# Transposing B, C, x and y of the state space heads through DMA, and writing TensorE's order by hand from the third chunk on

## The chip, the cores and the metric

The kernel runs on one core of one Trainium2 chip. The metric is the device time of one launch in microseconds (us). A core has TensorE (PE in the profile; its weight loads are PEld), VectorE (DVE), ScalarE (ACT), GpSimd (POOL) and SyncE (SP), each with an instruction queue of its own that it works off in order, and 16 DMA engines. In this kernel SP issues nearly every DMA, so its queue is also the order of the transfers. Tiles in SBUF are 128 partitions wide; matmul results go to PSUM.

## The reference, cut to what matters

One layer of a hybrid decoder on 256 tokens and 2048 features. The part that the change touches is the input projection and the state space (SSD) heads:

```
a_in = rmsnorm(h) ; proj = a_in @ w_in
z, xbc, dt_raw, q, k, v = split(proj)
xbc = silu(causal_dwconv(xbc))              # four taps along the tokens
xs, B, C = split(xbc)                       # 4 groups of 512 x channels, 128 of B, 128 of C
decay = exp(tril(a_cs[l] - a_cs[s]))
y_diag = (C B^T * decay) (xs * dt)          # per head, in chunks of 128 tokens
state  = B^T (xs * dt * decay_to_the_end)   # of the first chunk
y_off  = C state * exp(a_cs)                # of the second
y = (y_diag + y_off + d_skip * xs) * silu(z)
y_ssm = rmsnorm_per_group(y)
```

Then come sliding-window attention, one output projection over both groups of heads, a feed-forward layer with a convolution along the tokens, and a gated embedding.

## The kernel before, in words

All large products are made in three parts: weight and activation are split into a high and a low half (`wh`, `wl` and for instance `ah`, `al`), and high x high, high x low and low x high are summed. The unit of this work is a **step**: one weight tile of 256 x 512 against both blocks of 128 tokens, which is 12 products of 128x512 on PE (L219 to L221). For each step SP loads the tile `w` (L207), ACT makes `wh` of it (a cast, L192), and DVE makes `wl` (the "split", L193). `w` has seven buffers (`WR`), `wh` and `wl` have four (`WB`). So the split of step n can begin once PE has left step n-4, and the load of step n+7 once the split of step n is done.

The stages, in order of the program: 16 rounds with the B and C columns of the input projection (L317 to L319) and the products of `dt`; B and C are evacuated from PSUM with the row scale `rx`, transposed by PE so that channels lie on partitions (`conv_chunk`, L279), convolved by ACT and DVE (L266, L268) and put through SiLU. The function is then called for the x columns of each of the four groups. After the convolution of x, PE transposes back to tokens (L477); DVE makes `yc` = x d_skip and `Xd` = x dt from the transposed tile (L479, L482). The decays come as `seg` from a DRAM scratch (L442), one tile of 128x1024 for each of the two token chunks: DVE subtracts (L447), POOL masks (L448), ACT takes the exponential (L451), DVE multiplies by C B^T (L458). Then PE makes the state (L487), the eight heads of both chunks (L495) and the part from the state (L499); DVE sums into `yc` (L496 to L503). After the z columns of the group (`ssd_gate`), `ssd_end` gates, normalises and lets PE transpose `yc` once more (`transpose_split`, L252) to be the left operand of the output projection. The four groups are followed by attention, the rest of the output projection, the feed-forward layer and the gate.

Until the end of the four groups a scheduler sets the order of every engine from a simulated time line; with attention PE's order is written by hand (`manual_schedule`): a table gives the number of the step after which an event (scores, values) is put. The other engines' queues are set by the scheduler throughout. Attention and the feed-forward layer already transpose by DMA: `halves` splits 32-bit numbers into their two 16-bit halves, POOL copies them apart (`half`), SP issues a DMA transpose (`flip`), and POOL copies the halves together again.

Of the kernel before, what the change touches and what calls it, by code (L numbers as in the profile page):

```python
# [14 lines left out]
U16 = mybir.dt.uint16  # L15
AF = mybir.ActivationFunctionType
ALU = mybir.AluOpType
# [3 lines left out]
P = 128  # L21
# [44 lines left out]
def hybrid_layer(  # L66
# [205 lines left out]
    def conv_chunk(src, dst, cw, ntap, c0):  # L272

        for half in range(2):
            tr = tr_tile().rearrange("p (a t) -> p a t", a=2)
            for i in range(2):
                f = half * 2 + i
                for b in range(NB):
                    PE.transpose(tr[:, i, b * P : (b + 1) * P], src[b][:, f * P : (f + 1) * P], ident)  # L279
            for i in range(2):  # L280
                f = half * 2 + i
                w = cw[:, (c0 + f) * (ntap + 1) : (c0 + f + 1) * (ntap + 1)]
                conv_tile(tr[:, i, :], dst[:, f, :], [w[:, j : j + 1] for j in range(ntap)], w[:, ntap : ntap + 1])
# [59 lines left out]
    def in_chunk(c):  # L343
        acc = acc_pair()
        gemm(acc, aT, [w_in[c, g] for g in range(KT // KW)])
        return acc

    def evac_scaled(acc, pool, tag, bufs=None):
        res = []
        for b in range(NB):  # L350
            t = sb(pool, [P, NC], f"{tag}{b}", bufs=bufs)
            S.activation(out=t, in_=acc[b], func=AF.Copy, scale=rx[:, b : b + 1])
            res.append(t)
        return res
# [29 lines left out]
    with tc.tile_pool(name="ssd", bufs=1) as sp, tc.tile_pool(name="dram", bufs=1, space=bass.MemoryType.DRAM) as dp:  # L384
        BT = sb(sp, [P, 4, T], "BT")
        CT = sb(sp, [P, 4, T], "CT")
        for c, (acc, dst) in enumerate(((acc_b, BT), (acc_c, CT))):
            t = evac_scaled(acc, sp, "ct", 1)
            conv_chunk(t, dst, scw, 4, 16 + 4 * c)
            S.activation(out=dst, in_=dst, func=AF.Silu)  # L390

        tr = tr_tile()
        for b in range(NB):
            PE.matmul(tr[:, b * 32 : (b + 1) * 32], lhsT=dtT[:, b * P : (b + 1) * P], rhs=sel, start=True, stop=True)
        u = sb(sp, [P, 4, NB, 8], "dt_u")
        for b in range(NB):
            V.scalar_tensor_tensor(
                out=u[:, :, b, :], in0=v3(tr[:, b * 32 : (b + 1) * 32], 4), scalar=rx[:, b : b + 1], in1=v3(dtb, 4), op0=ALU.mult, op1=ALU.add
            )
        u = u.rearrange("p g c h -> p (g c h)")  # L400
        dt = sb(sp, [P, 64], "dt")
        e = sb(sp, [P, 64], "dt_e")
        e1 = sb(sp, [P, 64], "dt_e1")
        l1 = sb(sp, [P, 64], "dt_l1")
        V.scalar_tensor_tensor(out=e, in0=u, scalar=-1.0, in1=u, op0=ALU.mult, op1=ALU.min)
        S.activation(out=e, in_=e, func=AF.Exp)
        V.tensor_scalar_add(e1, e, 1.0)
        S.activation(out=l1, in_=e1, func=AF.Ln)
        V.scalar_tensor_tensor(out=e, in0=e1, scalar=-1.0, in1=e, op0=ALU.add, op1=ALU.subtract)
        V.reciprocal(e1, e1)  # L410
        V.tensor_tensor(out=e, in0=e, in1=e1, op=ALU.mult)
        V.scalar_tensor_tensor(out=dt, in0=u, scalar=0.0, in1=l1, op0=ALU.max, op1=ALU.add)
        V.tensor_tensor(out=dt, in0=dt, in1=e, op=ALU.subtract)
        dt4 = dt.rearrange("p (g c h) -> p g c h", g=4, c=NB)

        ea = sb(sp, [P, 32], "ea")
        S.activation(out=ea, in_=alog, func=AF.Exp)
        adt = sb(sp, [P, 64], "adt")
        adt4 = adt.rearrange("p (g c h) -> p g c h", g=4, c=NB)
        for b in range(NB):  # L420
            V.scalar_tensor_tensor(
                out=adt4[:, :, b, :], in0=dt4[:, :, b, :], scalar=-1.0, in1=v3(ea, 4), op0=ALU.mult, op1=ALU.mult
            )
        ps = ms_tile()
        PE.matmul(ps[:, :64], lhsT=triu, rhs=adt, start=True, stop=True)
        acs = sb(sp, [P, 64], "acs")
        V.tensor_copy(acs, ps[:, :64])
        ps = ms_tile()
        PE.matmul(ps[:64, :P], lhsT=adt, rhs=triu, start=True, stop=True)
        acsT = sb(sp, [64, P], "acsT")  # L430
        V.tensor_copy(acsT, ps[:64, :P])
        scr = dp.tile([64, P], F32, tag="scr", name="scr")
        nc.sync.dma_start(scr, acsT)
        eacs = sb(sp, [P, 64], "eacs")
        S.activation(out=eacs, in_=acs, func=AF.Exp)

        def ssd_x(g):
            segs = []
            for c in range(NB):
                hs = slice(g * 16 + c * 8, g * 16 + c * 8 + 8)  # L440
                seg = sb(sp, [P, 8, P], "seg", bufs=3)
                nc.sync.dma_start(seg, scr[hs, :].partition_broadcast(P))  # L442
                if c == 0:
                    dec = sb(sp, [P, 8], "dec", bufs=2)
                    V.tensor_tensor(out=dec, in0=seg[:, :, P - 1], in1=acs[:, hs], op=ALU.subtract)
                    S.activation(out=dec, in_=dec, func=AF.Exp)
# [5 lines left out]
                segs.append(seg)  # L452
            cb = ms_tile()
            for c in range(NB):
                cs = slice(c * P, (c + 1) * P)
                PE.matmul(cb[:, cs], lhsT=BT[:, g, cs], rhs=CT[:, g, cs], start=True, stop=True)
            for c in range(NB):
                V.tensor_tensor(  # L458
                    out=segs[c],
                    in0=segs[c],  # L460
                    in1=cb[:, c * P : (c + 1) * P].unsqueeze(1).to_broadcast([P, 8, P]),
                    op=ALU.mult,
                )
            tr = tr_tile()
            PE.transpose(tr[:, :P], BT[:, g, :P], ident)
            Bt = sb(sp, [P, P], "Bt", bufs=2)
            S.copy(Bt, tr[:, :P])

            t = evac_scaled(in_chunk(2 + 2 * g), sp, "ct", 1)
            xc = sb(sp, [P, 4, T], "xc")  # L470
            conv_chunk(t, xc, scw, 4, 4 * g)
            S.activation(out=xc, in_=xc, func=AF.Silu)
            y, Xd = [], []
            for b in range(NB):
                tr = tr_tile()
                for f in range(4):
                    PE.transpose(tr[:, f * P : (f + 1) * P], xc[:, f, b * P : (b + 1) * P], ident)  # L477
                yc = sb(sp, [P, NC], f"yc{b}", bufs=2)
                V.tensor_tensor(out=v3(yc, 8), in0=v3(tr, 8), in1=bc(dsk[:, g * 8 : (g + 1) * 8], HD), op=ALU.mult)  # L479
                y.append(yc)  # L480
                t = sb(sp, [P, NC], f"Xd{b}")
                V.tensor_tensor(out=v3(t, 8), in0=v3(tr, 8), in1=bc(dt4[:, g, b, :], HD), op=ALU.mult)  # L482
                Xd.append(t)
            xe = sb(sp, [P, NC], "xe")
            V.tensor_tensor(out=v3(xe, 8), in0=v3(Xd[0], 8), in1=bc(dec, HD), op=ALU.mult)
            st = ms_tile()
            PE.matmul(st, lhsT=Bt, rhs=xe, start=True, stop=True)  # L487
            prev = sb(sp, [P, NC], "prev")
            S.copy(prev, st)
            for c in range(NB):  # L490
                yc = y[c]
                yp = ms_tile()
                for h in range(8):
                    hs = slice(h * HD, (h + 1) * HD)
                    PE.matmul(yp[:, hs], lhsT=segs[c][:, h, :], rhs=Xd[c][:, hs], start=True, stop=True)  # L495
                V.tensor_tensor(out=yc, in0=yc, in1=yp, op=ALU.add)  # L496
                if c:
                    off = ms_tile()
                    PE.matmul(off, lhsT=CT[:, g, c * P : (c + 1) * P], rhs=prev, start=True, stop=True)  # L499
# [3 lines left out]
                    V.tensor_tensor(out=yc, in0=yc, in1=t, op=ALU.add)  # L503
            return y

        def ssd_gate(g):
            acc = in_chunk(3 + 2 * g)
            zs = []
            for b in range(NB):
                z = sb(sp, [P, NC], f"z{b}")  # L510
                S.activation(out=z, in_=acc[b], func=AF.Silu, scale=rx[:, b : b + 1])
                zs.append(z)
            return zs

        def ssd_end(g, y, zs):
            ssy = sb(sp, [P, NB], "ssy", bufs=2)
            for b in range(NB):
                V.tensor_tensor(out=y[b], in0=y[b], in1=zs[b], op=ALU.mult)
                S.activation(out=zs[b], in_=y[b], func=AF.Square, accum_out=ssy[:, b : b + 1])
            ry = rstd(ssy, NC, NB, "ry")  # L520
            for b in range(NB):
                V.tensor_scalar_mul(y[b], y[b], ry[:, b : b + 1])
            yT = Lhs(yp_, KG, "y")
            transpose_split(y, yT, 0, g_ssm[:, 4 * g : 4 * g + 4])
            return (yT, w_out, g, 1)

        y = ssd_x(0)
        zs = ssd_gate(0)

        with tc.tile_pool(name="rope", bufs=1) as rp:  # L530
            posf = sb(rp, [P, NB], "posf")
            V.tensor_copy(posf, posi)
            ang = sb(rp, [P, NB, HALF], "ang")
            for j in range(HALF):
                f = float(np.float32(THETA) ** np.float32(-2.0 * j / ROPE))
                V.tensor_scalar_mul(ang[:, :, j], posf, f)
# [416 lines left out]
```

## Time and profile before

| | us |
|---|---|
| time, median of 3 runs (lowest, highest) | 1434.91 (1434.77, 1435.49) |
| the profiled execution's own time | 1435.81 |
| its span | 1434.1 |
| ACT busy | 792.0 (55%) |
| POOL busy | 288.2 (20%) |
| B and C rounds and `dt` on PE end | at 55.4 |
| first and last head product of the four groups on PE | 127.3 and 304.7 |
| first scores of attention on PE | from 376.8 |

The profile is one execution. A row of a timeline gives start, duration, engine, line, operation and tiles; what stands in brackets is the idle time ahead of it and what ended it. Lines are those of the kernel before. The end of a matmul is modelled, so the pace of PE is read from the distance between starts.

### The profile page before, as it was taken

The numbers are of one execution on the slowest core, as the hardware profiler recorded it, in microseconds if no ns is written. First come the engines' busy times: TensorE is split into PE (matmuls) and PEld (weight loads), VectorE is DVE, ScalarE is ACT, GpSimd is POOL, SyncE is SP. The second block draws the span as 40 slices with busy tenths as digits, with TensorE's granted clock in tenths as the row PEclk, the third lists the DMA queues.
The fourth block names the chain that finished last, engine by engine and source line by source line (L and its number), as shares of the span: only waits on it lengthen the run. The fifth ranks groups of instructions, "written<-read, shape, count | busy, mean of one in ns | idle before, by whom it ended". The sixth has DMA issues, their size and how long they took to land.

```text
span 1434.1 us, 18053 instructions
## 1 busy us (share of the span) xinstructions
PE 1421.9 (99%) x6516; PEld 1166.2 (81%) x6516; DVE 995.0 (69%) x1240; ACT 792.0 (55%) x1067; POOL 288.2 (20%) x234
## 2 busy tenths in 40 slices
PE   9999999999999999999999999999999999999998
PEld 6887888888877777888888888888888888888886
DVE  6678876766789889656667646765675577476854
ACT  6575555544576655556556446545554554455643
POOL 0002010008535422013143103201320131120000
PEclk9999999999999999999999999999999999999999
DMA  9666656556787777577787777867876876776671
GB/s 338 217 190 202 201 177 189 163 160 205 191 236 198 213 203 223 171 208 209 217 231 198 217 196 216 228 194 202 226 208 194 221 214 205 206 207 190 209 223 66
DMA packets 163466, 292.62 MB, mean 204 GB/s; under 512 B 93040, under 2 KB 95920, under 8 KB 162992
## 3 DMA queue, kind: packets, MB, share of 16 engines
q1 hardware_dynamic: 162944, 290.99, 69.8%
q8 instruction: 51, 0.84, 0.2%
q10 hardware_dynamic: 432, 0.48, 0.1%
q14 instruction: 39, 0.32, 0.1%
HBM read 268.32 MB, written 2.13 MB: 189 GB/s over the span
## 4 chain that ended last, share of the span: by engine, by line
PE 61%; DVE 1%; issue 0%; ACT 0%; DVEq 0%
PE acc L220 20%; PE acc L221 20%; PE acc L219 20%; PE tr L252 0%; DVE wl L193 0%; PE tr L731 0%; DVE h L359 0%; DVE den L713 0%; DVE sg L883 0%; ACT s L709 0%; DVE yl L193 0%; DVE s L698 0%; DVE nm L705 0%; DVE sg L884 0%; ACT sg L882 0%
## 5 line engine op out<-in xcount | busy, mean ns | idle before, releaser
L193 DVE TENSOR_TENSOR wl<-w,wh 128x1024 fp32r<-128x1024 f32 (+1 forms) x493 | 637.8, 1298 | 370.9 <-ACT wh L192 370.1
L192 ACT CAST wh<-w 128x1024 fp32r<-128x1024 f32 (+1 forms) x493 | 514.8, 1049 | 496.6 <-PE acc L221 446.5
L220 PE MATMUL acc<-wl,ah 128*128 128x512 f32 x1280 | 499.8, 390 | 1.2 <-DVE wl L193 1.2
L221 PE MATMUL acc<-wh,al 128*128 128x512 f32 x1280 | 499.7, 391 | 0.0
L219 PE MATMUL acc<-wh,ah 128*128 128x512 f32 x1280 | 498.6, 391 | 0.0
L220 PEld LDWEIGHTS acc<-wl,ah 128*128 128x128 f32 x1280 | 240.4, 188 | 51.6 <-DVE wl L193 1.6
L219 PEld LDWEIGHTS acc<-wh,ah 128*128 128x128 f32 x1280 | 240.4, 188 | 50.8 <-issue 1.2
L221 PEld LDWEIGHTS acc<-wh,al 128*128 128x128 f32 x1280 | 240.4, 188 | 50.1 <-issue 0.5
L221 PE MATMUL acc<-wh,gl 128*128 128x512 f32 x352 | 137.0, 389 | 0.0
L220 PE MATMUL acc<-wl,gh 128*128 128x512 f32 x352 | 137.0, 389 | 0.0
L219 PE MATMUL acc<-wh,gh 128*128 128x512 f32 x352 | 136.4, 389 | 0.0
L833 POOL COPY half<-u 128x1024 uint16<-128x1024 uint16 x44 | 60.7, 1393 | 263.1 <-ACT u L831 263.1
L219 PE MATMUL acc<-wh,yh 128*128 128x512 f32 x256 | 101.3, 396 | 0.8 <-DVE h L359 0.8
L220 PE MATMUL acc<-wl,yh 128*128 128x512 f32 x256 | 100.0, 391 | 0.6 <-DVE wl L193 0.6
L221 PE MATMUL acc<-wh,yl 128*128 128x512 f32 x256 | 99.6, 390 | 0.0
L836 POOL COPY uc<-flip 128x1024 uint16<-128x1024 uint16 x44 | 55.7, 1265 | 166.3 <-DMA flip<-half 166.3
L220 PEld LDWEIGHTS acc<-wl,gh 128*128 128x128 f32 x352 | 66.1, 188 | 13.7
L221 PEld LDWEIGHTS acc<-wh,gl 128*128 128x128 f32 x352 | 66.1, 188 | 13.7
L219 PEld LDWEIGHTS acc<-wh,gh 128*128 128x128 f32 x352 | 66.1, 188 | 13.6
L359 DVE TENSOR_TENSOR h<-h,acc 128x512 f32<-128x512 f32 x112 | 72.6, 677 | 1.1 <-PE acc L221 1.1
L268 DVE SCALAR_TENSOR_TENSOR cv<-uc,fcw,cv 128x254 f32<-128x254 f32 (+1 forms) x176 | 73.0, 475 | 0.0
L219 PEld LDWEIGHTS acc<-wh,yh 128*128 128x128 f32 x256 | 48.0, 188 | 14.4 <-issue 4.3
(229 smaller groups left out, 1129.5 us busy)
## 6 DMA issues: line engine op xcount, KB each, us to landing
w<-in_w_up_dram SPq DMA_DIRECT2D x176, 512.0 KB, 3.9
w<-in_w_in_dram SPq DMA_DIRECT2D x126, 512.0 KB, 4.1
w<-in_w_down_dram SPq DMA_DIRECT2D x88, 512.0 KB, 4.2
w<-in_w_out_dram SPq DMA_DIRECT2D x64, 512.0 KB, 4.2
w<-in_w_pg_dram SPq DMA_DIRECT2D x32, 512.0 KB, 4.3
seg<-scr SPq DMA_DIRECT2D x8, 512.0 KB, 5.4
xt<-in_xT_dram SPq DMA_DIRECT2D x16, 128.0 KB, 6.5
h<-in_x_dram SPq DMA_DIRECT2D x2, 1024.0 KB, 8.6
```

Source lines behind the costliest of these rows:

```text
L192: S.copy(hi, src)
L193: V.tensor_tensor(out=lo, in0=src, in1=hi.bitcast(F32), op=ALU.subtract)
L219: PE.matmul(acc[b], lhsT=hi, rhs=wh[:, i, :], start=(k == 0), stop=False)
L220: PE.matmul(acc[b], lhsT=hi, rhs=wl[:, i, :], start=False, stop=False)
L221: PE.matmul(acc[b], lhsT=lo, rhs=wh[:, i, :], start=False, stop=(k == total - 1))
L268: V.scalar_tensor_tensor(out=dst[:, s:], in0=ps[:, : T - s], scalar=taps[n - 1 - s], in1=dst[:, s:], op0=ALU.mult, op1=ALU.add)
L359: V.tensor_tensor(out=hs, in0=hs, in1=acc[b], op=ALU.add)
L833: G.tensor_copy(half.rearrange("p (a n) -> p a n", a=2), u_.bitcast(U16).rearrange("p (n a) -> p a n", a=2))
L836: G.tensor_copy(uc[:, :, b * P : (b + 1) * P].bitcast(U16).rearrange("p f (t a) -> p f t a", a=2), flip.rearrange("p (a f) t -> p f t a", ...
```

## The change

It does three things.

First, `conv_chunk`'s and `ssd_x`'s transposes on PE, and those of `yc` in `transpose_split`, go. B, C, x (once to channels and once back) and y (to channels) are transposed through the path that attention has: per 128 tokens one POOL copy into 16-bit halves, one DMA transpose on SP and one POOL copy together (`transposed`, `together`, `to_channels`). The convolution, `Xd` and `y` now read SBUF instead of PSUM. `xa` holds the chunk, and its channels and its tokens are written over it in turn.

Second, `manual_schedule` for PE begins right behind the B and C rounds. `step` counts the steps from the first x chunk on; `plan` puts an event behind the products of a step. `chunk` and `output` move up from attention.

Third, a group's small products come in three visits: `decays_cb` (C B^T and the transpose of B), `state`, and `heads` (all 16 head products and the one from the state), 9, 16 and 18 steps behind the group's x chunk. `seg` has two buffers instead of three. The order of the parts becomes x and z of each group, the output projection of group 0, then q of the first heads.

```diff
-    def conv_chunk(src, dst, cw, ntap, c0):
...
-                    PE.transpose(tr[:, i, b * P : (b + 1) * P], src[b][:, f * P : (f + 1) * P], ident)
...
+    def transposed(pool, n, put):
+        half = sb(pool, [P, 2, n], "half", U16)
+        put(half)
+        flip = sb(pool, [P, 2 * n // P, P], "flip", U16)
+        nc.sync.dma_start_transpose(flip, half.rearrange("p a n -> p (a n)"))
+        return flip
+
+    def together(dst, flip):
+        G.tensor_copy(dst.bitcast(U16).rearrange("p c (t a) -> p c t a", a=2), flip.rearrange("p (a c) t -> p c t a", a=2))
...
+    def to_channels(pool, t):
+        flips = [
+            transposed(pool, NC, lambda half: G.tensor_copy(half, halves(t[:, b * NC : (b + 1) * NC]))) for b in range(NB)
+        ]
+        for b in range(NB):
+            together(v3(t, 4)[:, :, b * P : (b + 1) * P], flips[b])
...
+    def run(part):
+        for _ in part:
+            if step[0] in at:
+                for event in at[step[0]]:
+                    event()
+            step[0] += 1
...
+    order.enter_context(tc.manual_schedule(engines={PE.engine}))
...
-                seg = sb(sp, [P, 8, P], "seg", bufs=3)
+                seg = sb(sp2, [P, 8, P], "seg")
...
+        def ssd_x(g, acc):
+            t = scaled(acc, sp2)
+            to_channels(sp2, t)
+            xc = sb(sp, [P, 4, T], "xc")
+            convolve(v3(t, 4), xc, scw, 4, 4 * g)
             S.activation(out=xc, in_=xc, func=AF.Silu)
...
-                    PE.transpose(tr[:, f * P : (f + 1) * P], xc[:, f, b * P : (b + 1) * P], ident)
...
+                flipped(sp2, v3(tb, 4), NC,
...
+                d = sb(sp, [P, NC], f"Xd{b}")
+                V.tensor_tensor(out=v3(d, 8), in0=v3(tb, 8), in1=bc(dt4[:, g, b, :], HD), op=ALU.mult)
...
+        def state(g):
+            xe = sb(sp, [P, NC], "xe")
+            V.tensor_tensor(out=v3(xe, 8), in0=v3(xds[g][0], 8), in1=bc(segs[g][2], HD), op=ALU.mult)
+            st = tr_tile()
+            PE.matmul(st, lhsT=segs[g][3], rhs=xe, start=True, stop=True)
...
+        def heads(g):
...
+                    PE.matmul(yps[c][:, hs], lhsT=segs[g][c][:, h, :], rhs=xds[g][c][:, hs], start=True, stop=True)
+            PE.matmul(off, lhsT=CT[:, g, P : 2 * P], rhs=sts[g], start=True, stop=True)
...
-            transpose_split(y, yT, 0, g_ssm[:, 4 * g : 4 * g + 4])
+            to_channels(sp2, y)
...
+        plan(2, steps_dt)
+        plan(8, sums_dt)
+        plan(18, rotary)
+        for g in range(4):
+            end = 8 + 16 * g
+            plan(end + 4, lambda g=g: decays(g))
+            plan(end + 9, lambda g=g: decays_cb(g))
+            plan(end + 16, lambda g=g: state(g))
+            plan(end + 18, lambda g=g: heads(g))
+        for g in range(4):
+            run(chunk(2 + 2 * g, lambda acc: ssd_x(g, acc)))
+            run(chunk(3 + 2 * g, lambda acc: ssd_z(g, acc)))
+        run(output(0))
+        first_q = []
+        run(chunk(12, first_q.append))
```

How this moves instructions is shown at three places. The first is PE, in the last group. Before, this is the place of the state product (`ms` from `xe`) and of the first eight heads, which the scheduler put among the products of q:

```order
L220 MATMUL acc_524_2657<-wl_2732,ah_22_140 128x512
L487 MATMUL ms_2407<-xe_2405,Bt_2207 128x512
L495 MATMUL ms_2411<-Xd_460_2394,seg_2183 128x64 x8
L221 MATMUL acc_524_2657<-wh_2731,al_23_141 128x512
L219 MATMUL acc_523_2656<-wh_2731,ah_22_140 128x512
```

After, the state product of the last group (`tr` from `xe`) stands behind the products of step 72, and those of step 73 (`wh_2575`, `wl_2576`) stand behind it:

```order
L220 MATMUL acc_508_2549<-wl_2552,ah_18_136 128x512
L221 MATMUL acc_508_2549<-wh_2551,al_19_137 128x512
L572 MATMUL tr_2570<-xe_2568,Bt_2424 128x512
L219 MATMUL acc_507_2548<-wh_2575,ah_18_136 128x512
L220 MATMUL acc_507_2548<-wl_2576,ah_18_136 128x512
L221 MATMUL acc_507_2548<-wh_2575,al_19_137 128x512
```

So where PE reaches the row L572 before `xe` is there, it waits, with all products behind it.

The second place is SP's queue ahead of that product. Its rows are the loads of the weight tiles of steps 80 to 83 (`w_2852`, `w_2870`, `w_2888`, `w_2906`) and the DMA transposes of x of the last group back to tokens (`flip_2136` and `flip_2143`, one for each 128 tokens):

```order
L207 DMA w_2852<-in_w_in_dram 128x1024
L207 DMA w_2870<-in_w_in_dram 128x1024
L207 DMA w_2888<-in_w_in_dram 128x1024
L280 DMA_TRANSPOSE flip_2136<-half_2134 128x8x128
L207 DMA w_2906<-in_w_in_dram 128x1024
L280 DMA_TRANSPOSE flip_2143<-half_2141 128x8x128
```

There was no transfer here before; now `xe`, which is made from the tile that `flip_2136` fills, stands behind the load of step 82.

The third place is DVE. Before, around the heads of the third group, `seg` of the last group is taken up between the sums of `yc`, and splits stand in between:

```order
L496 TENSOR_TENSOR yc_374_1958<-yc_374_1958,ms_1977 128x512
L518 TENSOR_TENSOR yc_374_1958<-yc_374_1958,z_412_2148 128x512
L193 TENSOR_TENSOR wl_2339<-w_2337,wh_2338 128x1024
L447 TENSOR_TENSOR seg_2193<-seg_2193,acs_646 128x1024
L496 TENSOR_TENSOR yc_377_1967<-yc_377_1967,ms_1987 128x512
L502 TENSOR_TENSOR xe_1999<-ms_1997,eacs_654 128x512
```

After, with the heads of the same group, the rows are these (`dec` and `seg` belong to the last group; the split at the end is that of step 63):

```order
L589 TENSOR_TENSOR y_1701<-y_1701,ms_2214 128x512
L501 TENSOR_TENSOR dec_2306<-seg_2304,acs_625 128x8
L593 TENSOR_TENSOR xe_2237<-tr_2212,eacs_626 128x512
L503 TENSOR_TENSOR seg_2304<-seg_2304,acs_625 128x1024
L594 TENSOR_TENSOR y_1701<-y_1701,xe_2237 128x512
L503 TENSOR_TENSOR seg_2314<-seg_2314,acs_625 128x1024
L595 TENSOR_TENSOR y_1701<-y_1701,z_382_1945 128x512
L193 TENSOR_TENSOR wl_2359<-w_2357,wh_2358 128x1024
```

No split stands any more between the first row that needs the new `seg` and the last sum of `y`. Ahead of the row L572 DVE's queue reads as follows; the two splits are those of steps 75 and 76, and the first two rows add the output projection of group 0 to the residual, which needs the products of step 71:

```order
L372 TENSOR_TENSOR h_1_83<-h_1_83,acc_499_2508 128x512
L372 TENSOR_TENSOR h_2_84<-h_2_84,acc_500_2509 128x512
L193 TENSOR_TENSOR wl_2668<-w_2666,wh_2667 128x1024
L193 TENSOR_TENSOR wl_2686<-w_2684,wh_2685 128x1024
L549 TENSOR_TENSOR Xd_421_2139<-xa_2102,dt_623 128x512
L554 TENSOR_TENSOR y_2133<-xa_2102,rows_134 128x512
L570 TENSOR_TENSOR xe_2568<-Xd_421_2139,dec_2306 128x512
```

Before, `Xd` was made from PSUM right behind PE's own transposes; now it stands behind two more splits and behind the copy together of `flip_2136`.

More of the change, by code (lines that the diff above doesn't have):

```diff
@@ L393, in hybrid_layer @@
[L393 to L400, printed above, removed]
-        dt = sb(sp, [P, 64], "dt")
@@ L402, in hybrid_layer @@
[L402 to L411, printed above, removed]
```

413 lines of the change are left out of this document (212 added, 201 removed).

## The prediction

> **What bounds the kernel now.** I read the page's busy shares first, then the granted clock, then the chain of work that ended last.
>
> ```profile
> PE 1421.9 (99%) x6516; PEld 1166.2 (81%) x6516; DVE 995.0 (69%) x1240; ACT 792.0 (55%) x1067; POOL 288.2 (20%) x234
> PEclk9999999999999999999999999999999999999999
> PE 61%; DVE 1%; issue 0%; ACT 0%; DVEq 0%
> ```
>
> PE is the bound from end to end: 99% busy, at full granted clock, and nearly alone in the chain. So the time falls by whatever PE no longer does, and rises by whatever makes PE wait. The chain in order of time gives PE's pace:
>
> ```profile
> 592.00 0.87 PE tr L252 x8
> 617.43 0.45 PE acc L219 x2
> ```
>
> A transpose costs 0.87/8 = 0.109 us, a 128x512 product 0.45/2 = 0.226, a step of 12 products 2.72.
>
> **What goes.** The groups of PE that the change takes away:
>
> ```profile
> L279 PE MATMUL tr<-ident,ct 128*128 128x128 f32 x48 | 7.2, 272 | 1.1 <-ACT ct L352 1.1
> L477 PE MATMUL tr<-ident,xc 128*128 128x128 f32 x32 | 4.1, 272 | 0.0
> L252 PE MATMUL tr<-ident,yc 128*128 128x128 f32 x32 | 4.1, 272 | 0.0
> ```
>
> 48 + 32 + 32 = 112 transposes x 0.109 = **12.2 us**, all on the path, since PE has no gaps to hide them in. PE's timeline shows two waits in this stretch:
>
> ```profile
> 56.74 0.41 PE L279 MATMUL tr<-ident,ct 128*128 128x128 f32 x2 [1.09 <-ACT ct L352]
> 124.21 0.50 PE L220 MATMUL acc<-wl,ah 128*128 128x512 f32 x1 [1.15 <-DVE wl L193]
> ```
>
> The first goes: PE has products of the first x chunk to do while ACT evacuates, and ACT's new queue evacuates B's first tile two ACT instructions earlier. The second belongs to an old order that is gone; new waits are counted below. Together 2.2 us, so the gain is **14.5 us**. POOL's and DMA's new work (56 copies, 28 transposes) I cost at nothing in itself, because POOL is 20% busy; what it costs is latency, and that is the matter here. All other products, evacuations and splits stay.
>
> **What PE will wait for.** Before, the scheduler put the small products where their inputs were ready. Now they stand at fixed steps, so I work out when the inputs come. Three rates are needed. The first is how far splits run ahead (feed-forward layer, ACT and DVE):
>
> ```profile
> 636.51 1.05 ACT L192 CAST wh<-w 128x1024 fp32r<-128x1024 f32 x1 [1.67 <-PE acc L221]
> 637.60 1.23 DVE L193 TENSOR_TENSOR wl<-w,wh 128x1024 fp32r<-128x1024 f32 x1 [1.50 <-ACT wh L192]
> ```
>
> The cast starts when PE frees a buffer; the split ends at 638.83, 2.3 us later. With four buffers the split of step n ends 2.3 us after step n-4, and PE needs it 3 x 2.72 = 8.2 us after step n-4: a lead of 5.9 us. The second is a transpose by DMA, on SP and POOL:
>
> ```profile
> 634.41 1.47 SPq L835 DMA_TRANSPOSE flip<-half  x1
> 636.60 1.36 SPq L835 DMA_TRANSPOSE flip<-half  x1
> 638.99 1.17 POOL L836 COPY uc<-flip 128x1024 uint16<-128x1024 uint16 x1 [6.12 <-DMA flip<-half]
> 642.41 1.16 POOL L836 COPY uc<-flip 128x1024 uint16<-128x1024 uint16 x1 [2.26 <-DMA flip<-half]
> DMA to landing us min/median/max: 3.7/5.4/8.1
> ```
>
> From issue to POOL's copy 4.6 and 5.8 us, mean 5.2, and 1.2 for the copy. The third is DVE's own work, from its groups in 192 to 250 us:
>
> ```profile
> L193 DVE TENSOR_TENSOR wl<-w,wh 128x1024 fp32r<-128x1024 f32 x19 | 24.0, 1268 | 10.4 <-ACT wh L192 10.4
> L268 DVE SCALAR_TENSOR_TENSOR xc<-tr,scw,xc 128x255 f32<-128x255 f32 (+2 forms) x12 | 5.3, 476 | 0.1
> L458 DVE TENSOR_TENSOR seg<-seg,ms 128x1024 f32<-128x1024 f32 x2 | 2.3, 1204 | 0.0
> L482 DVE TENSOR_TENSOR Xd<-tr,dt 128x512 f32<-128x512 f32 x2 | 1.4, 680 | 0.0
> L522 DVE TENSOR_SCALAR yc<-yc,ry 128x512 f32<-128x512 f32 x2 | 0.9, 474 | 0.0
> ```
>
> (a) **The state product of the last group**, behind step 72. It needs `xe`, that `Xd`, that the copy together, that `flip_2136`, which stands in SP's queue behind the load of step 82. With seven landing buffers that load waits for the split of step 75, and with four split buffers that one waits for the end of step 71. So the transpose issues no sooner than 2.3 + 0.3 (DVE's two sums of `h`, 1.4 us, stand before the split, beside the cast of 1.05) + 0.35 (SP issues the load) = 3.0 us after step 71. Then 5.2 + 1.2, then `Xd`, `y` and `xe` at 0.68 each: 11.4 us after step 71. PE is there after 2.7. The wait is 8.7 us even if nothing else is late; with the shortest and the longest landing of the row it is 7 to 11.
>
> It will be more, as DVE is full there. From the split of step 67 to that of 75 it does 9 x 1.23 + 12 convolution parts x 0.476 + 8 sums of `h` x 0.68 + 2 x 1.2 of `seg` + 2 x 0.47 = 25.6 us in 9 steps of 2.72 = 24.5, without a moment of waiting; and it waits. The heads' place shows how (DVE, SP and ACT before):
>
> ```profile
> 188.00 4.43 SPq L442 DMA_DIRECT2D seg<-scr  x2
> 188.73 0.69 DVE L518 TENSOR_TENSOR yc<-yc,z 128x512 f32<-128x512 f32 x1
> 193.12 1.23 DVE L447 TENSOR_TENSOR seg<-seg,acs 128x1024 f32<-128x1024 f32 x1 [3.70 <-DMA seg<-scr]
> L451 ACT ACT_TABLE_LOAD x2 | 2.6, 1283 | 0.0
> ```
>
> `seg` waits until the heads have left its buffer, lands 5.1 us later (188.00 to 193.12), and DVE stands for 3.7 of it. In the new order, following the queues from the third group's heads with these durations, DVE loses 3 us to `seg` and about 4 waiting for ACT, which loads a function table (1.28) ahead of each change between exponential and SiLU. I get the last convolution part some 5 us after it could be done, and the SiLU, the 16-bit copies and the split of step 75 behind it late by as much. The wait is then about 14 us. Between 8.7 and 14 I take **12**, nearer to the upper, because DVE's sum alone exceeds its time.
>
> (b) **The state product of the third group**, behind step 56. Its transpose is issued in time (behind the load of step 63), but its `Xd` stands in DVE's queue behind the split of step 59, and ACT evacuates x of the last group (two of 0.69 us) ahead of that cast: 1.4 + 1.05 + 1.23 + 3 x 0.68 = 5.7 us after step 55, where PE arrives after 2.7. **3 us**; 1.6 if the evacuations come behind the cast. For the first two groups the same sum ends before PE arrives.
>
> (c) **The splits behind the heads**, three times. From the heads' end, `seg` lands after 5.2; `dec`, three sums and two subtractions (0.15 + 3 x 0.68 + 2 x 1.22) end at 9.9, the next split at 11.1. PE has four steps in stock, 10.9. So about 0.2, and up to 2 where ACT is behind as well; before, one such place in four gave the 1.15 us above. 0 to 6 in all; I take **3**.
>
> (d) **The clock.** A pause of 12 us is new. The trace shows slow matmuls only behind PE's idle start:
>
> ```profile
> 6.00:9.00 3.00, 2.38 (x7) 1.80 (x7) 1.32 (x4) 2.32 (x4) 0.00 (x0) 0.66 1.02 341
> 9.00:12.00 3.00, 3.00 (x12) 2.43 (x11) 1.94 (x3) 1.64 (x4) 0.00 (x0) 0.78 1.02 343
> ```
>
> The granted clock (third number from the end) cost 3 x 0.34 + 3 x 0.22 = 1.7 us there. No pause in mid-run is long enough to show whether it does this. Between 0 and 1.7 I take **1.7**, the only row there is. [...]
>
> **Sum.** -14.5 + 12 + 3 + 3 + 1.7 = +5.2 us on the profiled execution's own 1435.8 (its span is 1434.1, with 1.7 around it): 1441.0. That execution is 0.9 above the median of the runs shown, so the forecast is **1440** as a median.
>
> **Rivals.**
>
> *The queues keep up (faster).* DVE and ACT catch up, since both have idle time before (69% and 55% busy), (b), (c) and (d) vanish, and (a) shrinks to its floor: -14.5 + 8 = -6.5, 1428.4. It decides at 14.5 us of waits in all. For it: no row shows the new order, and SP's rows show a lot of stock in the loads. Against it: the floor of (a) hangs on buffers and queue order alone, and DVE's 42.55 us of work per group (next row) meet steps that take 46.
>
> ```profile
> 192.00:250.00 58.00, 58.00 (x284) 48.10 (x284) 42.55 (x54) 32.32 (x43) 4.07 (x3) 1.00 0.60 183
> ```
>
> *Gain and waits cancel.* (a) at 9 to 11, 2 to 4 for the rest: within 3 us of 1435.
>
> *DVE becomes the bound.* That row holds 19 splits; with 16 a group takes 42.55 - 3 x 1.23 = 38.9 us of 46 (16 steps and the small products). Output and q add on, and POOL's copies beside it may stretch splits (mean 1.268 against 1.23 undisturbed). If each of three group ends loses 3 us and (a) 14, it is 14 + 3 + 9 + 1.7 - 14.5 = +13.2: 1448.
>
> *The change doesn't do what it says: the transposes starve PE of weights.* Each holds SP for 1.4 us and waits there for POOL. For 28 it would be up to 39 us if loads were late. Against it stands SP's largest wait:
>
> ```profile
> SPq L207 <- DVE wl L193: 961.2, 437, 9.0
> ```
>
> SP waits 961 us in all for a landing buffer, so the loads have stock. I leave it 0.03.
>
> **How the numbers follow.** My forecast, with (a) at 11 to 14: 0.40, its own range 1438 to 1445. Faster rival 0.25, cancelling 0.20, DVE bound 0.12, starving 0.03. A measurement of this kernel can tell some 0.2% (2.9 us) from no change: below 1432.0 is faster, 0.25; between, 0.20; above 1437.8, 0.40 + 0.12 + 0.03 = 0.55 slower. The bounds of the terms give -14.5 + 7 = -7.5 (1427.4) and -14.5 + 14 + 3.3 + 6 + 1.7 = +10.5 (1445.4), and the DVE rival reaches a little beyond: 1427 to 1447 holds 8 in 10.
>
> **What would show it.** PE's waits by cause: one of 9 to 14 us at the state product of the last group, released by DVE's `xe`, with `flip` issued about 3 us or more after step 71; one of about 3 at the third group's; several of 1 to 2 on splits behind the heads. A granted clock below 1 right behind the long wait, or none, settles (d). The transposes' groups of 48, 32 and 32 gone, and starts of products still 0.226 apart, settle the gain. The forecast is wrong if `flip` of the last x lands before step 72 ends, which would need SP to be past the load of step 82 earlier than the split buffers allow, or if the chunk's waits add up to less than 14.5.

## The result and the profile after

| | before | after |
|---|---|---|
| time, median (lowest to highest), us | 1435.2 (1434.77 to 1436.87) | 1459.8 (1456.97 to 1460.27) |
| the profiled execution's own time, us | 1435.81 | 1460.27 |
| its span, us | 1434.1 | 1458.5 |

The ratio is 1.0165, with a 95% interval of 1.0147 to 1.0183. The change makes the kernel slower, as forecast, but by 24.6 us and not by 5.

The page of the kernel after shows in its busy shares, its row of PE's busy tenths, its row of the granted clock and its chain:

```profile
PE 1419.7 (97%) x6404; PEld 1156.4 (79%) x6404; DVE 1035.3 (71%) x1240; ACT 793.7 (54%) x1070; POOL 377.0 (26%) x290
PE   9999998969999999999999999999999999999998
PEclk9999999989999999999999999999999999999999
PE 60%; DVE 1%; issue 0%; DMA 0%; ACT 0%; DVEq 0%
```

112 instructions are gone from PE, yet its busy time has hardly fallen, and slices 7 and 9 of the 40 have holes (36 us each; the seventh begins at 219, the ninth at 292). In slice 9 the granted clock is below 0.9, which no slice had before. PE's waits by cause (us in all, times, longest) name the holes:

```profile
PE tr L572 <- DVE xe L570: 20.5, 3, 13.1
PE acc L220 <- DVE wl L193: 8.4, 9, 3.3
PE acc L336 <- ACT wh L192: 1.6, 2, 0.9
PE acc L219 <- DVE h L372: 1.2, 3, 0.7
```

Where the time is lost can be read from the starts of the same step in both traces (the first product of the step, after minus before; from step 88 on, keys behind q, both kernels have done the same work):

| step | 88 | 112 | 128 | 150 | 192 | 470 |
|---|---|---|---|---|---|---|
| after minus before, us | +16.4 | +17.4 | +23.6 | +24.5 | +24.5 | +24.5 |

So 16.4 us are lost in the SSD part, another 8.1 in attention, and nothing behind it. The prediction had looked for waits in the SSD part only.

The timeline of PE after shows the two long waits of the SSD part and what stands behind the second one:

```profile
237.43 2.08 PE L572 MATMUL tr<-xe,Bt 128*128 128x512 f32 x2 [5.79 <-DVE xe L570]
...
304.60 2.08 PE L572 MATMUL tr<-xe,Bt 128*128 128x512 f32 x2 [13.11 <-DVE xe L570]
305.68 1.42 PE L219 MATMUL acc<-wh,ah 128*128 128x512 f32 x1
306.89 0.63 PE L220 MATMUL acc<-wl,ah 128*128 128x512 f32 x1
307.32 0.48 PE L221 MATMUL acc<-wh,al 128*128 128x512 f32 x1
307.64 0.39 PE L219 MATMUL acc<-wh,ah 128*128 128x512 f32 x1
307.87 0.40 PE L220 MATMUL acc<-wl,ah 128*128 128x512 f32 x1
```

Behind the wait the starts lie 1.21, 0.43 and 0.32 us apart before they reach 0.23: PE is slow. The windows of the same trace (last numbers: granted clock, DMA share, GB/s) give the clock there, and behind a wait of 3.3 us in attention:

```profile
305.00:308.00 3.00, 3.00 (x7) 1.71 (x7) 2.54 (x2) 0.58 (x1) 1.93 (x2) 0.58 0.00 0
308.00:311.00 3.00, 3.00 (x15) 2.45 (x14) 0.00 (x0) 1.05 (x1) 0.00 (x0) 1.00 0.00 0
453.00:456.00 3.00, 1.82 (x5) 1.44 (x6) 3.00 (x3) 2.97 (x6) 0.05 (x1) 0.71 0.11 37
```

Why is `xe` so late? POOL's timeline after, around x of the last group, whose evacuation by ACT ends at 229.65:

```profile
231.19 1.67 POOL L284 COPY xa<-flip 128x1024 uint16<-128x1024 uint16 x1 [3.86 <-DMA flip<-half]
232.80 1.04 POOL L293 COPY half<-y 128x1024 uint16<-128x1024 uint16 x1
...
243.51 1.04 POOL L293 COPY half<-xa 128x1024 uint16<-128x1024 uint16 x1 [6.68 <-DMA flip<-half]
...
254.81 1.90 POOL L284 COPY y<-flip 128x1024 uint16<-128x1024 uint16 x1 [9.16 <-DMA flip<-half]
256.67 1.50 POOL L293 COPY half<-xa 128x1024 uint16<-128x1024 uint16 x1
```

The two copies of the last x into halves start 14 and 27 us after the evacuation, though POOL stands idle ahead of the first for 6.68 us. What they wait for is a buffer: `half` and `flip` have two each, which are handed out in the order of the program. That order is x of the group to channels, x back to tokens, then y of the group before. So the last x stands behind y of group 1, and that behind x of group 2 on its way back (231.19). Its SiLU comes at 290.86, 1.1 us long, and ACT's cast for step 75 and with it the load of step 82 and `flip_2136` (294.52) come behind it, as rows of ACT's and of SP's timeline show:

```profile
290.86 1.06 ACT L534 ACTIVATE xc<-xc 128x1024 f32<-128x1024 f32 x1
294.52 1.24 SPq L280 DMA_TRANSPOSE flip<-half  x1
```

The path from there to `xe` is longer than its instructions were before. DVE's `Xd` and `xe` (min/median/max in ns) are these:

```profile
L549 DVE TENSOR_TENSOR Xd<-xa,dt x8: 678/1491/1521, 127.8 to 304.5; 128x512 f32<-128x512 f32 x8
L570 DVE TENSOR_TENSOR xe<-Xd,dec x4: 683/1518/1632, 129.0 to 302.9; 128x512 f32<-128x512 f32 x4
```

The shortest are as forecast, the median is twice as long. Beside each of the eight that took 1.4 us or more POOL was at work for 0.95 us or more, beside the four short ones for 0.25 us at most.

This gives two theories. **Shared buffers:** x's transposes are late because y's use the same two buffers, and PE's fixed places turn that into waits. **Queue order**, the prediction's: the transpose stands behind loads that follow PE, and DVE is full, so the wait has a floor of 8.7 us whatever the buffers are. For attention the theory is a **late start**: its tiles take the place of the SSD tiles, and the last of these is y of the last group, which now goes through DMA.

### The profile page after: what moved, and what is told of

Read it like the earlier page. It is cut to its first block, busy times and chain, and to the rows that moved or that the text cites. A ratio compares the mean times of both kernels' runs of the same rounds, so it can differ in the third digit from the quotient of the medians.

```text
span 1458.5 us, 17921 instructions
## 1 busy us (share of the span) xinstructions
PE 1419.7 (97%) x6404; PEld 1156.4 (79%) x6404; DVE 1035.3 (71%) x1240; ACT 793.7 (54%) x1070; POOL 377.0 (26%) x290
## 3 DMA queue, kind: packets, MB, share of 16 engines
HBM read 268.32 MB, written 2.13 MB: 185 GB/s over the span
## 4 chain that ended last, share of the span: by engine, by line
PE 60%; DVE 1%; issue 0%; DMA 0%; ACT 0%; DVEq 0%
PE acc L220 20%; PE acc L219 20%; PE acc L221 20%; PE tr L252 0%; DMA w<-in_w_out_dram 0%; DVE wl L193 0%; PE tr L808 0%; ACT s L786 0%; DVE sg L935 0%; DVE yl L193 0%; DVE s L775 0%; DVE nm L782 0%; DVE sg L936 0%; DVE h L372 0%; ACT sg L934 0%
## 5 line engine op out<-in xcount | busy, mean ns | idle before, releaser
L193 DVE TENSOR_TENSOR wl<-w,wh 128x1024 fp32r<-128x1024 f32 (+1 forms) x493 | 651.8, 1329 | 360.5 <-ACT wh L192 359.3
L219 PE MATMUL acc<-wh,ah 128*128 128x512 f32 x1280 | 504.0, 395 | 0.6 <-DVE h L372 0.6
```

What stands on the lines that cost most here:

```text
L193: V.tensor_tensor(out=lo, in0=src, in1=hi.bitcast(F32), op=ALU.subtract)
L219: PE.matmul(acc[b], lhsT=hi, rhs=wh[:, i, :], start=(k == 0), stop=False)
```

## The experiments

Where a ratio is given, it is to the kernel before, in runs on the same chip (medians 1436.1 to 1436.5). The changed kernel's 1459.8 was measured beside a median of 1435.2, so a difference to it can be off by some 1.3 us.

### Buffers of its own for y

```diff
-    def transposed(pool, n, put):
-        half = sb(pool, [P, 2, n], "half", U16)
+    def transposed(pool, n, put, own="", bufs=None):
+        half = sb(pool, [P, 2, n], "half" + own, U16, bufs)
...
-            to_channels(sp2, y)
+            to_channels(sp2, y, "_y", 1)
```

> The transposes of y get a half and a flip buffer of their own, one each, so that only x to channels and x back share the two old ones. Theory of the buffers: in the changed kernel x of the last group waits for a half buffer behind y of group 1, and that one behind x of group 2 going back, because all three pass the same two buffers in the order of the program. Then xe of the third and last groups is in time here: the waits of 5.8 and 13.1 us at the state products fall below 2 us each, no slow clock stands behind them, and the time falls by about 17 to 22 us to 1438 to 1443. Theory of the prediction (the last load of step 82 ahead of the transpose, and DVE full): the wait at the last state product stays at 9 us or more and the time above 1452.

Measured: 1443.15 us, ratio 1.0047 (1.003 to 1.0063). POOL's timeline of this kernel has the last x copied into halves 4 us after its evacuation (ending at 230.90), both parts in one go:

```profile
234.68 2.94 POOL L293 COPY half<-xa 128x1024 uint16<-128x1024 uint16 x2
```

ACT's timeline has SiLU of it 26 us earlier than after the change:

```profile
264.84 1.06 ACT L534 ACTIVATE xc<-xc 128x1024 f32<-128x1024 f32 x1 [2.11 <-DVE xc L268]
```

And PE's largest waits are these:

```profile
PE acc L220 <- DVE wl L193: 6.8, 9, 2.1
PE tr L572 <- DVE xe L570: 3.3, 2, 2.4
PE sc L771 <- POOL kT L284: 3.0, 1, 3.0
```

The waits for `xe` fall from 20.5 to 3.3 us, and step 88 starts 2.6 us before that of the kernel before instead of 16.4 behind it. The theory of the shared buffers holds, and the floor of 8.7 us falls: in this kernel's SP queue the first transpose of the last x back to tokens (272.52) stands behind the load of step 76 and not of step 82. The queue order from which the floor was worked out came itself from the shared buffers. Attention still loses 11 us between steps 88 and 192, so the late start is another matter. Since y has one `half` buffer here, the two halves of the last y even pass one after the other (POOL copies them at 302.64 and 313.94).

### Later places for the state products and heads

```diff
-            plan(end + 16, lambda g=g: state(g))
-            plan(end + 18, lambda g=g: heads(g))
+            plan(end + (16, 16, 19, 21)[g], lambda g=g: state(g))
+            plan(end + (18, 18, 21, 23)[g], lambda g=g: heads(g))
```

> Only the places on PE are moved: state product and heads of the third group 3 steps later (behind steps 59 and 61), those of the last group 5 steps later (behind steps 77 and 79). If the lost time is only PE standing at a place that came too early, the waits of 5.8 and 13.1 us shrink to 0 to 3 us, the slow products behind them (some 3 us) go too, and the time falls to 1438 to 1441. Rival: attention begins when y of the last group is transposed; then its vector work falls back against PE by as much as the heads were moved, the waits in attention (6.3 us at steps whose split is late, and 1.8 us of slow clock) grow to 12 us or more, and the time is 1444 to 1452.

Measured: 1450.55 us, ratio 1.0101 (1.0086 to 1.0116): the rival's range. The wait of 5.8 us is gone, that of 13.1 is 4.4, and step 88 is only 1.3 us late. But attention then loses 14 us more. Moving the places without moving the work hands the loss on.

### The last y by PE

```diff
+            if g == 3:
+                plan(78, lambda: by_pe(y))
+                return
             to_channels(sp2, y)
```

> Only y of the last group goes back to PE's transposes, 8 of them behind step 78 (0.9 us); everything else is as in the changed kernel. If attention's waits come from its late start behind the DMA transposes of that y, the first rope work of q on POOL starts 8 us earlier against PE's steps (346.9 us in the changed kernel), PE's waits between 400 and 600 us fall from 6.3 to 2 us, the slow clock at 454 us goes, and the time falls by 4 to 6 us to 1453 to 1456. If they come from the order of DVE or POOL in attention itself, the time stays at 1458 to 1461.

Measured: 1453.84 us, ratio 1.0122 (1.0106 to 1.0137), 6.0 us less than the changed kernel. POOL's first work of attention comes at 335.05 instead of 346.88. PE's waits by cause between 400 and 600 us, in the changed kernel (6.8 us in all, where the expectation counted 6.3):

```profile
PE acc L220 <- DVE wl L193: 4.9, 3, 3.3
PE acc L219 <- ACT wh L192: 1.0, 1, 1.0
PE acc L219 <- DVE h L372: 0.9, 2, 0.7
```

The same in this one:

```profile
PE acc L220 <- DVE wl L193: 1.7, 3, 0.9
```

Step 88 is 19.2 us late here, step 470 is 19.7: attention loses 0.5 us instead of 8.1. So the DMA transposes of the last y cost attention 7.6 of the 8.1 us.

That the link is the late start is borne out by all 14 kernels of this case. How far ahead of PE's step 88 POOL's first work of attention starts (the `rs` of L187) goes with what attention then loses between steps 88 and 192 against the kernel before:

| kernels | start ahead of step 88, us | attention's loss, us |
|---|---|---|
| before, and the seven with the last y by PE | 14.2 to 20.1 | -1.1 to 3.3 |
| 22 unused products (below) | 7.0 | 5.5 |
| after; 14 unused products (below) | 5.4; 5.4 | 8.1; 8.3 |
| buffers of its own for y | 4.2 | 11.1 |
| later places; PE's order by the scheduler (below) | 2.5 behind; 2.5 behind | 14.0; 17.0 |

### Both repairs together

> Both repairs together: y has its own half and flip buffer, and y of the last group is transposed by PE behind step 78. If the two losses are separate (xe late through the shared buffers, attention late through the last y), the gains add: from 1459.8 the 16.7 us of the own buffers and the 6.0 us of the last y give 1437; and since own buffers alone left 7.9 us of waits and about 3 us of slow clock in attention, it may reach 1433 to 1437. If the two are one and the same lateness, the second repair adds less than 3 us: 1440 to 1443.

Measured: 1433.23 us (1430.15 to 1437.5, 10 runs), ratio 0.998 (0.9969 to 0.9991). The gains add, and a little more: 26.6 us below the changed kernel, where 16.7 and 6.0 make 22.7. The result is faster than both kernels, if only by 0.2% against the kernel before. The busy shares of its page:

```profile
PE 1413.6 (99%) x6412; PEld 1154.4 (81%) x6412; DVE 1032.2 (72%) x1240; ACT 793.2 (55%) x1068; POOL 364.7 (25%) x286
```

Its largest waits of PE, which now add up to 12.5 us in all:

```profile
PE acc L220 <- DVE wl L193: 4.6, 7, 2.1
PE tr L572 <- DVE xe L570: 4.3, 2, 2.5
```

### All y by PE, in two places

As the last y above, for every group: at first 4 steps behind the heads.

> All four y go back to PE's transposes (32, some 3.1 us in all, 4 steps behind the heads); B, C and x stay on DMA, half and flip keep their two buffers. If y in the shared buffers and the late last y are the cause of nearly all that was lost, this is as good as the two repairs together less 2.3 us for the 24 transposes more: 1435 to 1440, with waits at the state products below 3 us. If x's own path (copy, transfer, copy, convolution, copy, transfer, copy) is too long for its place in any case, waits of 5 us or more stay there and the time is above 1445.

Measured: 1454.75 us, ratio 1.013 (1.0114 to 1.0146). The time is that of the second expectation, but not by its cause: y no longer passes the buffers, and `xe` costs 1.7 us in all. But a new wait stands at the transposes, which came before DVE had normalised y, as PE's waits by cause show:

```profile
PE tr L252 <- DVE y L605: 17.9, 4, 7.7
```

With these transposes 4 steps later in groups 0 to 2:

> As the run with all y by PE, whose transposes came up to 7.7 us too early in groups 0 to 2; they now stand 4 steps (10.9 us) later there. If only that place was wrong, PE's waits at these transposes (2.8, 0.5, 7.0 and 7.7 us) and the slow clock behind them go, and the time falls from 1454.8 by 18 to 20 us to 1434 to 1438. If x's transfers have only profited from PE standing there, waits of 3 us or more come back at the state products and the time is above 1442.

Measured: 1439.77 us, ratio 1.0031 (1.0018 to 1.0043). The wait is gone, the time fell by 15.0 and not 18 to 20: step 88 starts 1.2 us before that of the kernel before, but 3.2 us come back in attention. So B, C and x on DMA with y on PE are 20 us better than the changed kernel, but no better than the kernel before or than both repairs together.

### Small moves around the repaired kernel

Four experiments asked what else could be had. Three buffers for the decays (`bufs=3` at `seg`), on top of all y by PE:

> As the run before, with three buffers for the decays instead of two, as the kernel before the change had. If DVE stands behind the heads because the decays of the next group wait for the heads to leave their buffer (term c), the waits for splits behind the heads (at about 117 to 160 us and 205 to 275 us) halve and the time falls by 1 to 3 us. If those waits come from DVE's own work, it is the same within 1 us.

Measured: 1448.41 us, ratio 1.0084 (1.0071 to 1.0097): slower by 8.6. The last convolution of x in group 0 moved behind other work on DVE, and PE waits 7.8 us for that group's `xe`. Whether DVE stood for `seg` (term c) is not told by this, as the scheduler changed the order of all queues.

Both repairs with every group's state product and heads one step later, and with the state products of groups 0 and 3 alone one step later:

> As both repairs together, and state product and heads of every group one step later (17 and 19 steps behind the x chunk, y of the last group behind step 79). What was left at the state products (1.0 us in group 0, 2.4 in the last) goes: 2 to 3 us below the run with both repairs. If the late splits behind the heads grow in its place, or attention waits for the later heads, it is the same within 1.5 us or slower.

> Both repairs, and the state products of groups 0 and 3 alone one step later (the heads stay). PE's two waits for xe (1.8 and 2.5 us) go, nothing behind them moves, since the heads keep their place: 1433.2 less 3 to 4 us, 1429 to 1431. If the heads then wait for the state's evacuation, or DVE is late by the same at the next split, it is 1432 to 1434.

Measured: 1441.8 us, ratio 1.0037 (1.0023 to 1.0051), and 1438.98 us (1430.7 to 1442.38, 12 runs), ratio 1.0015 (1.0003 to 1.0027). Neither is faster than both repairs alone, and both expectations of a gain failed. In the first PE waits 4.5 us at step 66 for ACT's evacuation of z and 3.4 us for a split behind the heads of group 0. In the second the wait for the last `xe` grew from 2.5 to 4.0 us although PE came later. SP's timeline shows why. With both repairs the first transpose of the last x back to tokens is issued here:

```profile
270.80 1.24 SPq L280 DMA_TRANSPOSE flip<-half  x1
```

With the state products moved it is issued here:

```profile
278.74 1.24 SPq L280 DMA_TRANSPOSE flip<-half  x1
```

That is 7.9 us later. PE itself is 5.0 us later by then (its step 66 starts at 266.93 instead of 261.93), with a wait of 3.6 us for a split behind the heads of group 0 (2.1 with both repairs). The transpose also stands behind one load more, that of step 77 instead of 76, which is a step of 2.7 us. The loads wait for split buffers that PE frees, so the two traces fit this part of the prediction's mechanism, that the transfers follow PE's pace; no run isolates it.

Last, PE's order in the SSD part left to the scheduler (`manual_schedule` begins with attention):

> PE's order in the SSD part is left to the scheduler again (written by hand only from attention on); transposes by DMA, three visits, buffers and the order of the parts as in the changed kernel. If the hand-written places are what makes PE wait, the state products move to where the scheduler expects xe, the waits of 5.8 and 13.1 us shrink to less than 5 in all and the time is 1440 to 1448 (attention still late). If the scheduler expects the transfers much earlier than they come, or keeps these places, the waits stay at 15 us or more and the time is 1455 to 1462.

Measured: 1450.81 us, ratio 1.0099 (1.0082 to 1.0116), between the two expectations. No wait for `xe` is left, and step 88 starts 1.6 us before that of the kernel before: without the places written by hand the late x costs PE nothing in the SSD part. But attention then loses 17.0 us, so only 9 us of the time are won. PE's waits by cause are now those of attention and of splits:

```profile
PE acc L220 <- DVE wl L193: 9.6, 9, 2.4
PE sc L771 <- POOL kT L284: 5.9, 1, 5.9
PE acc L219 <- ACT qkr L709: 3.4, 1, 3.4
```

### PE kept busy in the pause

```diff
+            if g == 3:
+                idle = ms_tile()
+                for _ in range(22):
+                    PE.matmul(idle, lhsT=ident, rhs=sts[2], start=True, stop=True)
             st = tr_tile()
```

> 22 products of 128x512 f32 (0.54 us each at full clock, 11.9 us in all; their result is not used) stand ahead of the state product of the last group, in PE's 13.1 us of waiting. If the granted clock follows PE's own idle time, the products behind that state product start 0.227 us apart at once (in the changed kernel the first five take 1.21, 0.43 and so on at a clock of 0.5), and about 1.5 us are saved: 1456 to 1459. If the clock fell for another reason, those products stay slow and the time is that of the changed kernel, 1457 to 1460.

> As the first run with unused products ahead of the last state product, of which each took 0.86 us there and not 0.54, so that they lasted 18.9 us; 14 of them now, 12.0 us, inside the wait of 13.1. PE then waits for xe some 1 us, the products behind it start 0.23 us apart at once, and the time falls by 1 to 2 us against the changed kernel, to 1456 to 1459.

Measured: 1459.54 and 1459.85 us, one run each. The 22 products took 18.9 us, 0.86 each and not 0.54, and overran the pause, so the time tells nothing, but the clock does. PE's timeline of the run with 22, behind the state product:

```profile
308.01 1.02 PE L576 MATMUL tr<-xe,Bt 128*128 128x512 f32 x2
308.47 0.79 PE L219 MATMUL acc<-wh,ah 128*128 128x512 f32 x1
309.10 0.39 PE L220 MATMUL acc<-wl,ah 128*128 128x512 f32 x1
309.33 0.40 PE L221 MATMUL acc<-wh,al 128*128 128x512 f32 x1
```

The same place of the run with 14, where 2.45 us of waiting were left:

```profile
303.79 1.60 PE L576 MATMUL tr<-xe,Bt 128*128 128x512 f32 x2 [2.45 <-DVE xe L570]
304.40 1.41 PE L219 MATMUL acc<-wh,ah 128*128 128x512 f32 x1
305.62 0.63 PE L220 MATMUL acc<-wl,ah 128*128 128x512 f32 x1
306.04 0.63 PE L221 MATMUL acc<-wh,al 128*128 128x512 f32 x1
```

Without a pause, the products behind the state product start 0.23 us apart at once (but for the first step of 0.63, which stands behind the first group's state product too), and the granted clock is 1.00 (308 to 311 us). Behind 2.45 us of waiting they are slow (1.22, 0.42, 0.43), and the clock is 0.55 (304 to 307 us). At this place the clock fell with PE's pause and stayed at 1.00 without it.

## Why the prediction was right and wrong, point by point

**The sign was right, the size wrong.** The forecast was +5.2 us against the profiled execution, and 24.5 came. The largest step that failed is "All other products, evacuations and splits stay": it puts attention at nothing, and attention lost 8.1 us. The others are the clock (5.5 us against 1.7), the third group's state product (5.8 against 3) and the first group's (1.6 against nothing).

**The gain (14.5) held.** The transposes were priced at 0.109 each, 12.2 in all. From the start of each to the start of the next instruction on PE they took 4.3 (L279), 3.2 (L477) and 3.1 us (L252) in the trace of before, 10.6 in all: within a row the starts lie 0.11 us apart, but behind each of the 20 rows the next product starts 0.03 us after the last transpose. That product is followed only after 0.31 or 0.32 us instead of 0.23, which makes 1.7 us over the 20 rows and 12.3 with them. The two waits (1.09 and 1.15) went, as forecast; the new ones for splits are counted under (c).

**(a) held: 13.1 us, against 12.** `flip_2136` was issued behind the load of step 82, at 294.52, and PE's waiting began at 291.49. But its floor of 8.7 us was no floor: with other buffers the transpose stands behind an earlier load, and the wait is 2.4. The lateness of the last x, which the prediction put down to DVE's full queue and the function tables, began at 229.65 with a wait for `half`.

**(b) failed: 5.8 us, against 3.** Most of it is "3 x 0.68": `Xd`, `y` and `xe` took 1.49, 1.63 and 1.52, 4.5 us from first to last instead of 2.04, as POOL copied beside them. So POOL's new work, put at "nothing in itself", had a price. The rest is the transposed x. SiLU of x of group 2 came at 221.14, and its first transpose was issued at 225.37, behind the load of step 63 as forecast. But POOL's copy began 5.8 us after that and took 1.67, where (a) had counted 5.2 and 1.2; it ended at 232.86, 1.0 us later than the split of step 59 (231.85) that was held to be the last thing. "In time" had no margin. With buffers of its own for y this wait is gone. The state product of the first group, for which no wait was counted, waited 1.58.

**(c) was about right: 2.3 us, against 3**, as waits of 1.30, 0.30 and 0.70 for splits behind the heads of three groups. Two more of 0.68 (for a split at 117.18, ahead of the first heads) and 0.35 (for a sum of `h`) are of another kind, and so was the example from before: its wait of 1.15 ends at 124.21, ahead of the first head product at 127.3. Ahead of the split of the 0.70 DVE stood for `seg` for 2.80 us (until 253.80), close to the 3 us forecast, but no run isolates `seg` as the cause.

**(d) was sized for one place, where it held.** Compared with the same 14 instructions behind the first group's state product (3.73 us), those behind the pauses of 5.8 and 13.1 us took 6.19 and 5.12: 2.5 and 1.4 us lost. Another 1.6 went behind the 3.3 us in attention (12 instructions, 4.44 against 2.85). That is 5.5 us, against 1.7; the pause that had been priced cost 1.4. Whether a pause in mid-run lowers the clock, which no row of before had shown, the kernel after answers: the granted clock was 0.50 from 237 to 240 us, behind the 5.8 us, and 0.50 from 303 to 306, around the end of the 13.1. With 14 unused products a pause of 2.45 us was enough (0.55).

**Attention was left out, and cost 8.1 us.** "All other products, evacuations and splits stay" was true of the instructions and not of their times. The last y is ready for attention's tiles only after two transfers and four copies (its last copy starts at 337.56), so ACT, DVE and POOL begin attention late, and the splits behind it come late too. Of the 8.1 us, 4.9 are waits (6.8 against 1.9) and 1.6 slow clock; the last 1.6 were not followed.

**The balance.** Waits of PE: 33.6 us against 6.95, +26.6 in all. Slow clock +5.5, transposes -12.3. Together +19.8 of the 24.4; the remaining 4.6 us are spread over the first products behind waits and small products and were not followed further.

**The rivals.** DVE as the bound gave 1448 and came nearest, but DVE is 71% busy and no sum of its work sets the time. That the queues keep up came true only with the two repairs, at 1433.2 instead of 1428.4 (a sum that used 8 us for the floor of 8.7). Gain and waits did not cancel. The transposes did not starve PE of weights: ACT's casts waited 5.7 us in all for loads of `w_in`, and 7.6 before.

## What to carry to other kernels

When transposes move from PE to DMA, count the staging buffers and write down the order in which their users get them; a user that is in no hurry (y) must not stand in the same line as one on the critical path (x). A wait at a fixed place is worth moving only if what it waits for does not follow PE itself, and what the moved work releases (here the start of the next stage) has to be followed as well. Price an operation beside its new neighbours (`Xd` took 0.68 us alone and 1.49 beside POOL's copies), and a pause of PE with the slow stretch behind it (all 26 pauses from 2.19 us up had one here).

## What the runs showed of the hardware

**Behind pauses of PE from about 2 us up its products were slow.** In the kernel after the granted clock was 1.00 from 159 to 162 us, behind a pause of 1.30 us, 0.71 from 453 to 456 around the end of one of 3.32, and 0.50 from 237 to 240 behind one of 5.79. In the 14 profiled executions of this case, behind their first 15 us, 51 pauses of PE from 0.7 to 1.83 us, standing alone, were followed by products 0.23 us apart; of nine from 1.85 to 2.13 us, seven were followed by products 0.43 us apart; of 26 from 2.19 us up, all. Two pauses of 0.85 and 0.76 us with 0.5 us of work between them were also followed by slow products. The slow stretch lasts 1 to 11 products and does not follow the length of the pause (one behind 13.11 us, seven behind 1.85), and sometimes begins a few products after it: behind one of 1.86 us four products started 0.23 to 0.34 apart, and only then 0.41 and 0.43.

**DVE operations with two operands in SBUF and POOL's copies took longer beside each other.** In the kernel after, `Xd` and `xe` take 0.68 us alone and up to 1.63 beside a POOL copy; the splits of 128x1024 take 1.22 us without POOL (mean of 315) and 1.58 where POOL is busy throughout (mean of 45). POOL's copies of x into halves take 1.04 us alone and up to 2.04. DVE's operation is not always longer: the `y` at 302.31 takes its 0.68 us though POOL copies beside it for 0.58; that copy, which goes on beside the `xe` of 1.63, takes 1.59 instead of 1.15. The sums of `h`, which read one operand from PSUM, take 0.68 us in both cases (73 and 22 of them). By what mechanism the two slow each other, and why the sums of `h` are spared, is not shown by any run.
